# Moving Silus, RG-LRU scans and step-size work within the instruction stream of a hybrid SSD / RG-LRU block

## The chip, the cores and the metric

One core of a Trainium2 chip runs the whole layer as one launch. The metric is the device time of one execution in microseconds (us). The five engines are TensorE (PE), VectorE (DVE), ScalarE (ACT), GpSimd (POOL, idle here) and SyncE (SP, which issues the DMAs). Each engine works through its own instructions in order; semaphores hold an instruction until what it reads is there and what it overwrites has been read.

## What is computed

One layer over 256 latent tokens and 256 context tokens, with 2048 channels, in float32. The normalised and modulated input `h` goes through one projection that is split among two mixers, and both mixers run forwards and backwards:

```python
z, xs, bs, cs, dt_raw, xr, yr = jnp.split(h @ lp['w_in'], IN_SPLITS, axis=-1)
# (A) Mamba-2 SSD: conv + silu of xs, bs, cs; dt = softplus(dt_raw + bias); A = -exp(a_log)
a_cum = jnp.cumsum(dt * A, axis=2)                       # per head and chunk of 128
y_diag = einsum(CB * exp(a_cum_i - a_cum_j), xdt)
y_off  = einsum(C, exp(a_cum), entering_state)
# (B) RG-LRU: r, i = sigmoid(block-diagonal products of conv(xr))
a = exp(-8 * r * softplus(-lam));  u = sqrt(-expm1(2 log a)) * (i * xr);  h_t = a_t h_{t-1} + u_t
```

Then `rmsnorm(y * silu(z))` and `r * gelu(yr)` go through output projections, sigmoid gates merge them, and after one more projection and a gated residual comes a SwiGLU feed-forward network. Context tokens are only needed for the states from which the latent scans start.

## The kernel before

Channels lie on the 128 partitions, tokens in the free dimension: columns 0 to 255 are latent, 256 to 511 context. Almost every product is a *job* (`Job`, line 46): one 128-column tile of a weight matrix, sixteen k-tiles, loaded by DMA in two pieces (`load`, line 150), split by ACT (line 173) and DVE (line 174) into a high and a low part (`parts`, line 164), and multiplied by PE in three passes (`product`, line 177). A ring of four raw and four split pieces runs ahead of PE. A job in the mode "both" has all 512 columns, one in the mode "lat" the 256 latent ones.

PE's order is written out by hand. `run` (line 249) goes through the jobs; behind each job come, in this order: its evacuation (`job.evac`), the next weight pieces, and then the functions that were put off to this place: first those in `turns[0]`, then one `step()` of the queue `bg`. `in_turn(n, f)` called from an evacuation puts `f` behind the n-th job after that one, with n = 0 behind the same job; called from inside a turn, n = 0 is the next job. The order of the other engines is chosen by a list scheduler from the program order and its own estimate of times, with one exception: `fn` (line 105) chains all ACT functions that need a table (Exp, Tanh, Sigmoid, Sqrt, Silu, Gelu) in the order in which the program emits them, so an early one that isn't ready holds all later ones back. ACT loads another table (ACT_TABLE_LOAD) where neighbours of that chain belong to different sets; Exp and Tanh share one here.

Four pieces of this stream matter:

**RG-LRU.** The sixteen channel tiles are handled in eight pairs. `lru_batch` (line 509) puts five steps per pair into `bg`, one behind each job, the fifth together with the next pair's first: `operands(t0)`; the *previous* pair's `scans` (the list `before`); `gates(t0)` and `operands(t1)`; nothing; `gates(t1)` and `decays`. So pair p has its steps behind jobs 4p to 4p+4. `gates` (line 528) issues twelve matmuls into four PSUM banks (lines 535 to 537, tile `lg`), each bank read by one Sigmoid (line 538); the banks of the two directions come from two pools of two and three banks (`lru_ps`, `ssd_ps`), so that a tile's gates need those of the tile before to be read. `decays` are eight Exp and Tanh and six DVE instructions (lines 547 to 550), `scans` (line 552) two Sqrts on ACT, then ten DVE instructions (lines 559 to 565) and two DMAs to `rD`.

**Step sizes.** `dt_evac` (line 598), the evacuation of job 0, computes softplus, cumulative sums and decay weights for 64 heads. `steps(0)` is for the latent tokens, `steps(1)` for the context. Each is a chain of some 30 small instructions on DVE (log1p by a series, lines 132 to 146, then scans, line 614) with one Exp at its head (line 136) and one at its end (line 634 or 641); `turn` (line 645) transposes the results on PE into `wt`, and for part 0 makes `dec` with one more Exp. `steps(0)` is emitted at job 0, its turn and all of `steps(1)` at job 4 (ahead of that job's `step()`), the second turn at job 9.

**SSD.** After the first 34 jobs come four groups of six jobs in the order xs0, C, xs1, B, xs2, xs3 (C is "lat", the others "both"), then 32 gate jobs less those already done, then the z jobs. When a group's xs3 is evacuated (`xs_evac`, line 695), the group's Silus (`silus`, line 723: B, C and the 2048 columns of XS) are emitted, and the rest of its work is put into turns: three context steps, and four *units* (`unit`, line 788), each of a `fetch` (a DMA that broadcasts the cumulative sums from DRAM, line 795, tile AC with two buffers), `operands` (lines 798 to 817: ACT line 804 and DVE line 805 make E, Exp of AC and E, then DVE makes G, line 816) and `products` (PE, line 833, 24 matmuls of 128 columns):

```python
LONG = ((1, 2, 3), (4, 5, 6, 7), (2, 3, 4, 5), (3, 4, 5, 6))       # line 692: context, products, fetch, operands
SHORT = ((2, 3, 5), (7, 9, 11, 13), (4, 6, 7, 9), (5, 7, 9, 11))
```

In groups 0 to 2 the last unit's `operands` are behind the sixth job after xs3. That is the next group's xs3, in whose evacuation the next group's Silus have just been emitted. The last unit's `products` follow one job later, and right behind them comes the next group's `context_tokens` (line 739): transposes of B (`pB`), B times C (`pC`), transposes of XS (`px`, line 736). For group 2 the two jobs after group 3's xs3 are "lat" gate jobs, and with SHORT group 3's `context_tokens` stand behind the second.

Of the kernel before, what the change touches and what calls it, by code (L numbers as in the profile page):

```python
# [10 lines left out]
AF = mybir.ActivationFunctionType  # L11
ALU = mybir.AluOpType
PSUM = bass.MemoryType.PSUM

P = 128
# [4 lines left out]
NG = 4  # L20
# [35 lines left out]
def hybrid_block(  # L56
# [450 lines left out]
    before = []  # L507

    def lru_batch(tiles):
        st = {}  # L510

        def new(name, t):
            st[name, t] = lp.tile([P, 2, 2 * T], F32, tag=name, name=name, bufs=4 if name == "I" else 2)
            return st[name, t]

        def operands(t):

            raw = lp.tile([P, 4, P], F32, tag="lw", name="lw", bufs=1)
            side.dma_start(raw.rearrange("p a b -> p (a b)"), lru_w[t])
            w = [lp.tile([P, 4, P], F32R, tag=n, name=n, bufs=1) for n in ("lh", "ll")]  # L520
            x = [lp.tile([P, 2 * T], F32R, tag=n, name=n, bufs=1) for n in ("xh", "xl")]
            act.copy(w[0], raw)
            dve.tensor_sub(w[1], raw, w[0].bitcast(F32))
            act.copy(x[0], xcs[t])
            dve.tensor_sub(x[1], xcs[t], x[0].bitcast(F32))
            st["op", t] = w, x

        def gates(t):
            R, I = new("R", t), new("I", t)
            (wh, wl), (xh, xl) = st["op", t]  # L530
            for d in range(2):
                for g, (dst, bn) in enumerate(((R, "lba"), (I, "lbx"))):
                    ps = (lru_ps, ssd_ps)[d]("lg")
                    q = 2 * d + g
                    pe.matmul(ps, wh[:, q], xh, start=True, stop=False)  # L535
                    pe.matmul(ps, wh[:, q], xl, start=False, stop=False)
                    pe.matmul(ps, wl[:, q], xh, start=False, stop=True)
                    fn(dst[:, d, :], ps, AF.Sigmoid, bias=col(bn, 16 * d + t))

        def decays():  # L540
            for t in tiles:
                R, I, A, E = st["R", t], st["I", t], new("A", t), new("E", t)
                for d in range(2):
                    n = 16 * d + t
                    fn(A[:, d, :], R[:, d, :], AF.Exp, scale=SL[:, 0, n:n + 1])
                    fn(R[:, d, :], R[:, d, :], AF.Tanh, scale=SL[:, 1, n:n + 1])
                dve.tensor_tensor(E, A, A, ALU.mult)

                dve.scalar_tensor_tensor(E, E, 1.0, R, ALU.add, ALU.mult)
                dve.tensor_tensor(I, I, xcs[t].unsqueeze(1).broadcast_to([P, 2, 2 * T]), ALU.mult)  # L550

        def scans():
            for t in tiles:
                E = st["E", t]
                fn(E, E, AF.Sqrt, bias=epsb[:, 1:2])
            lat, con = slice(0, T), slice(T, 2 * T)
            for t in tiles:
                I, A, E = (st[k, t] for k in "IAE")
                dve.tensor_tensor(I, I, E, ALU.mult)
                dve.tensor_tensor_scan(E[:, 0, con], A[:, 0, con], I[:, 0, con], 0.0, ALU.mult, ALU.add)  # L560
                dve.tensor_tensor_scan(E[:, 0, lat], A[:, 0, lat], I[:, 0, lat],
                                       E[:, 0, 2 * T - 1:2 * T], ALU.mult, ALU.add)
                dve.tensor_tensor_scan(E[:, 1, ::-1], A[:, 1, ::-1], I[:, 1, ::-1], 0.0, ALU.mult, ALU.add)
                ro = tp.tile([P, T], F32, tag="hv", name="ro", bufs=4)
                dve.tensor_tensor(ro.rearrange("p (r c) -> p c r", r=ROWS),
                                  E[:, 0, lat].rearrange("p (c r) -> p c r", r=ROWS),
                                  E[:, 1, lat].rearrange("p (c r) -> p c r", r=ROWS), ALU.add)
                side.dma_start(rD[t], ro)
                del xcs[t]


        t0, t1 = tiles
        todo = [(False, [lambda: operands(t0)]), (False, before[:]), (False, [lambda: gates(t0), lambda: operands(t1)]),
                (False, []), (True, [lambda: gates(t1), decays])]
        before[:] = [scans]
        if tiles[1] == KT - 1:
            todo.append((False, [scans]))
        return todo
# [19 lines left out]
    def dt_evac(ps):  # L598
# [13 lines left out]
        def steps(part):  # L612
            def scan(o, i, n, pr):
                dve.tensor_tensor_scan(o, ones2[pr, :n], i, 0.0, ALU.mult, ALU.add)

            t0, t1, t2, dt = (dp.tile([64, T], F32, tag=f"dt{i}", name=f"dt{i}") for i in range(4))
            da = x[:, part * T:part * T + T]
            log1p_exp(dt, da, (t0, t1, t2))
            dve.tensor_scalar(da, dt, na, None, ALU.mult)
            ones2, ex, ac = t0, t1, t2  # L620
            dve.memset(ones2, 1.0)

            dve.memset(ex, 0.0)
            if part == 0:
                for c in range(2):
                    s = slice(c * P, c * P + P)
                    scan(ac[f, s], da[f, s], P, f)
                    scan(ac[b, s][:, ::-1], da[b, s][:, ::-1], P, b)
                scan(ex[f, 0:P - 1][:, ::-1], da[f, 1:P][:, ::-1], P - 1, f)
                scan(ex[b, 1:P], da[b, P:2 * P - 1], P - 1, b)  # L630
                for c in range(2):
                    for d, pr in enumerate((f, b)):
                        side.dma_start(acD[c, d], ac[pr, c * P:c * P + P])
                fn(ex[:, :P], ex[:, :P], AF.Exp)
                dve.tensor_tensor(ex[f, :P], ex[f, :P], dt[f, 0:P], ALU.mult)
                dve.tensor_tensor(ex[b, :P], ex[b, :P], dt[b, P:2 * P], ALU.mult)
                cols = (dt[:, :P], dt[:, P:], ac[:, :P], ac[:, P:], ex[:, :P])
            else:
                scan(ex[f, :T - 1][:, ::-1], da[f, 1:][:, ::-1], T - 1, f)
                scan(ex[b, 1:], da[b, :T - 1], T - 1, b)  # L640
                fn(ex, ex, AF.Exp)
                dve.tensor_tensor(ex, ex, dt, ALU.mult)
                cols = (ex[:, :P], ex[:, P:])

            def turn():
                pt = ssd_ps("pt")
                for i, src in enumerate(cols):
                    pe.transpose(pt[:, 64 * i:64 * i + 64], src, ident[:64, :64])
                o = 5 * part
                act.copy(wt[:, o:o + len(cols)].rearrange("p a b -> p (a b)"), pt[:, :len(cols) * 64])  # L650
                if part == 0:
                    dve.tensor_scalar(wt[:, 2:4], wt[:, 2:4], -1.0, None, ALU.mult)
                    dg = dp.tile([64, 64], F32, name="dg")
                    dve.tensor_scalar(dg[f], ident[f, :64], ac[f, P - 1:P], None, ALU.mult)
                    dve.tensor_scalar(dg[b], ident[b, :64], ac[b, P:P + 1], None, ALU.mult)
                    pd = ssd_ps("pd")
                    pe.matmul(pd[:, :64], ones[:64], dg, start=True, stop=True)
                    fn(dec, pd[:, :64], AF.Exp)
            return turn

        def first():
            turn0()
            in_turn(4, steps(1))

        turn0 = steps(0)
        in_turn(4, first)

    def start_ssd():
        flush()
# [19 lines left out]

    LONG = ((1, 2, 3), (4, 5, 6, 7), (2, 3, 4, 5), (3, 4, 5, 6))
    SHORT = ((2, 3, 5), (7, 9, 11, 13), (4, 6, 7, 9), (5, 7, 9, 11))

    def xs_evac(g, t):
        def f(ps):
            if (g, t) == (0, 0):
                start_ssd()
            if t == 0:
                sd["XS"] = sd["gp"].tile([P, 4, 2 * T], F32, tag="XS", name="XS", bufs=2)  # L700
            i = 4 * g + t
            conv(ps, sd["XS"][:, t, :].rearrange("p (s t) -> p s t", s=2), col("cw", 4 * i, 4), col("cb", i), 2)
            if t == 3:
                silus, *rest = ssd_group(g)
                silus()
                for ns, fs in zip(LONG if g < NG - 1 else SHORT, rest):
                    for n, part in zip(ns, fs):
                        in_turn(n, part)
        return f

    def ssd_group(g):
# [130 lines left out]
            return products, fetch, operands  # L842

        units = [unit(u, c) for u in range(2) for c in range(2)]
        return (silus, [context_tokens, context_states, carried_states], *zip(*units))

    jobs = [Job(w_dt, KT, "narrow", None, dt_evac)]
    for t in range(N0, KT):
# [155 lines left out]
    first = []  # L1004
# [118 lines left out]
```

## Time and profile before

| | us |
|---|---|
| median of 3 runs | 2028.81 (2024.41 to 2029.35) |
| the profiled execution, own time | 2027.59 |
| its span, first to last instruction | 2025.8 |
| mean granted TensorE clock | 0.986 of full speed |
| PE busy | 1963.7 (97%) |
| DVE busy | 1430.7 (71%) |
| ACT busy | 1088.2 (54%) |

A busy PE is the normal state: what can be won without changing the products is the time in which PE stands, and the time in which it runs at a lower granted clock. In the rows below a line of the timeline gives start and duration in us, engine, line of the kernel, operation, output<-inputs, shape and count; a bracket gives the idle time of that engine just before it and what ended it.

### The profile page before, as it was taken

What the parts mean: (1) busy time and instruction counts of PE and PEld (TensorE: products, weight loads), DVE (VectorE), ACT (ScalarE), POOL (GpSimd) and SP (SyncE); (2) the same over time, 40 slices, a digit from 0 to 9 for tenths busy, and PEclk for the clock granted to TensorE, in tenths of its full rate; (3) what the DMA queues carried; (4) which work ended last, traced back from release to release, by engine and by line L of the source; (5) the groups of instructions that cost most, each with busy time, mean ns of one, the idle gap of its engine ahead of it and who ended that gap; (6) DMA issues with size and microseconds to landing.
All of it is one profiled execution on the core that took longest, in us unless ns stands there. A gap on an engine that the chain in (4) does not pass through costs nothing.

```text
span 2025.8 us, 30510 instructions
## 1 busy us (share of the span) xinstructions
PE 1963.7 (97%) x11633; PEld 1691.9 (84%) x11633; DVE 1430.7 (71%) x2153; ACT 1088.2 (54%) x1652; POOL 0.2 (0%) x4
## 2 busy tenths in 40 slices
PE   7999899999999879999999999899999999999997
PEld 3778898898878769888888888788888888888887
DVE  5578989886776666888777878776666665545544
ACT  4245878684564454766655544554444444444442
POOL 0000000000000000000000000000000000000000
PEclk9999999999999989999999999999999999999999
DMA  9974354556454457899888877577777776666663
GB/s 371 358 271 144 122 160 132 170 170 199 140 160 143 138 164 228 264 315 360 290 274 274 271 249 254 175 249 232 231 241 237 230 230 189 184 188 186 185 193 122
DMA packets 143842, 440.32 MB, mean 217 GB/s; under 512 B 17488, under 2 KB 36176, under 8 KB 143568
## 3 DMA queue, kind: packets, MB, share of 16 engines
q1 hardware_dynamic: 143328, 437.91, 66.4%
q8 instruction: 91, 1.49, 0.3%
q10 hardware_dynamic: 368, 0.47, 0.1%
q14 instruction: 55, 0.45, 0.1%
HBM read 427.77 MB, written 10.55 MB: 216 GB/s over the span
## 4 chain that ended last, share of the span: by engine, by line
PE 92%; DMA 2%; DVE 2%; ACT 2%; issue 1%; SPq 0%; DVEq 0%; ACTq 0%
PE ps L206 36%; PE ps L209 19%; PE ps L188 5%; PE ps L189 5%; PE ps L190 5%; PE ps L192 3%; PE ps L193 3%; PE ps L194 3%; DMA AC<-acD 1%; PE ps L391 1%; PE pa L344 1%; PE ps L392 1%; PE py L833 1%; PE ps L393 1%; PE ps L228 1%; PE lg L535 1%
## 5 line engine op out<-in xcount | busy, mean ns | idle before, releaser
L174 DVE TENSOR_TENSOR wl<-raw,wh 128x1024 fp32r<-128x1024 f32 (+1 forms) x566 | 677.8, 1200 | 386.9 <-ACT wh L173 382.3
L173 ACT CAST wh<-raw 128x1024 fp32r<-128x1024 f32 (+1 forms) x566 | 581.0, 1030 | 646.8 <-issue 221.4
L206 PE MATMUL ps<-T,wh 128*128 128x512 f32 x3236 | 814.7, 393 | 0.0
L206 PEld LDWEIGHTS ps<-T,wh 128*128 128x128 f32 x3236 | 581.6, 189 | 105.2 <-issue 0.7
L209 PEld LDWEIGHTS ps<-T,wl 128*128 128x128 f32 x3236 | 442.7, 190 | 33.3
L209 PE MATMUL ps<-T,wl 128*128 128x256 f32 x3236 | 452.9, 282 | 0.0
L188 PE MATMUL ps<-T,wh 128*128 128x512 f32 x464 | 184.2, 397 | 0.0
L189 PE MATMUL ps<-T,wh 128*128 128x512 f32 x464 | 180.9, 390 | 0.0
L190 PE MATMUL ps<-T,wl 128*128 128x512 f32 x464 | 180.6, 389 | 0.0
L473 DVE SCALAR_TENSOR_TENSOR rawa<-rawa,sc 128x1024 f32<-128x1024 f32 x128 | 153.1, 1222 | 28.4 <-DMA rawa<-in_dram 28.1
L192 PE MATMUL ps<-T,wh 128*128 128x256 f32 x576 | 165.4, 287 | 0.0
L193 PE MATMUL ps<-T,wh 128*128 128x256 f32 x576 | 163.7, 284 | 0.0
L194 PE MATMUL ps<-T,wl 128*128 128x256 f32 x576 | 163.6, 284 | 0.0
L192 PEld LDWEIGHTS ps<-T,wh 128*128 128x128 f32 x576 | 111.3, 193 | 1.9 <-issue 0.7
L193 PEld LDWEIGHTS ps<-T,wh 128*128 128x128 f32 x576 | 111.4, 193 | 1.2 <-issue 0.5
L194 PEld LDWEIGHTS ps<-T,wl 128*128 128x128 f32 x576 | 111.2, 193 | 0.0
L188 PEld LDWEIGHTS ps<-T,wh 128*128 128x128 f32 x464 | 87.1, 188 | 20.5 <-issue 2.3
L189 PEld LDWEIGHTS ps<-T,wh 128*128 128x128 f32 x464 | 87.2, 188 | 18.9 <-issue 1.4
L190 PEld LDWEIGHTS ps<-T,wl 128*128 128x128 f32 x464 | 87.1, 188 | 18.5
L107 ACT ACT_TABLE_LOAD x48 | 61.6, 1283 | 0.8
L804 ACT ACTIVATE E<-AC,wt 128x128 f32<-128x128 f32 x64 | 20.6, 391 | 61.8 <-DMA AC<-acD 61.8
L385 DVE TENSOR_TENSOR wl<-raw,wh 128x896 fp32r<-128x896 f32 x16 | 17.5, 1092 | 45.1 <-ACT wh L384 45.1
(236 smaller groups left out, 1881.8 us busy)
## 6 DMA issues: line engine op xcount, KB each, us to landing
raw<-in_dram SPq DMA_DIRECT2D x534, 512.0 KB, 4.5
rawa<-in_dram SPq DMA_DIRECT2D x128, 512.0 KB, 5.9
wa<-in_dram SPq DMA_DIRECT2D x64, 512.0 KB, 7.2
AC<-acD SPq DMA_DIRECT2D x16, 512.0 KB, 6.6
raw<-in_dram SPq DMA_DIRECT2D x16, 448.0 KB, 7.1
raw<-in_dram SPq DMA_DIRECT2D x16, 384.0 KB, 3.3
raw<-in_dram SPq DMA_DIRECT2D x18, 256.0 KB, 2.7
X<-in_dram SPq DMA_DIRECT2D x8, 512.0 KB, 7.2
```

The costliest lines, as they stand in the source:

```text
L107: i = act.activation(dst, src, func, **kw).ins
L173: act.copy(h[:, :n], raw[:, :n])
L174: held["low"] = dve.tensor_sub(l[:, :n], raw[:, :n], h[:, :n].bitcast(F32)).ins
L188: pe.matmul(ps, wh, T1[:, k, :], start=s, stop=False)
L189: pe.matmul(ps, wh, T2[:, k, :], start=False, stop=False)
L190: pe.matmul(ps, wl, T1[:, k, :], start=False, stop=e)
L192: pe.matmul(ps[:, :T], wh, T1[:, k, :T], start=s, stop=False)
L193: pe.matmul(ps[:, :T], wh, T2[:, k, :T], start=False, stop=False)
L194: pe.matmul(ps[:, :T], wl, T1[:, k, :T], start=False, stop=e)
L206: pe.matmul(ps, wh, job.act(k), start=s, stop=False, skip_group_check=True)
L209: pe.matmul(ps[:, T:], l[:, i % KP, :], job.act(i)[:, :T], start=False, stop=i == last, skip_group_check=True)
L473: i = dve.scalar_tensor_tensor(raw, raw, 1.0, sc[:, h * 1024:h * 1024 + 1024], ALU.mult, ALU.mult, accum_out=MP[:, n, h:h + 1]).ins
```

## The change

The Silus of a group are no longer emitted in the evacuation of xs3 but in a turn with n = 0, behind whatever already stands in that job's turns (for groups 1 to 3 the last unit's `operands`). The scans of a pair go from the second step of the next pair to its third, behind `gates(t0)` and `operands(t1)`. The step-size work is in four turns per run through: `steps(0)` at job 1, its closing Exp and multiplications (`weights`) at job 3, its `turn` at job 5; `steps(1)` at job 7, `weights` at job 9, `turn` at job 11. The last unit of group 2 has its products at the eighth job after xs3 in place of the seventh (`LAST_LONG`), just ahead of group 3's `context_tokens`.

```diff
@@ -570,8 +570,8 @@
 
 
         t0, t1 = tiles
-        todo = [(False, [lambda: operands(t0)]), (False, before[:]), (False, [lambda: gates(t0), lambda: operands(t1)]),
-                (False, []), (True, [lambda: gates(t1), decays])]
+        todo = [(False, [lambda: operands(t0)]), (False, []),
+                (False, [lambda: gates(t0), lambda: operands(t1)] + before), (False, []), (True, [lambda: gates(t1), decays])]
         before[:] = [scans]
         if tiles[1] == KT - 1:
             todo.append((False, [scans]))
@@ -631,16 +631,20 @@
                 for c in range(2):
                     for d, pr in enumerate((f, b)):
                         side.dma_start(acD[c, d], ac[pr, c * P:c * P + P])
-                fn(ex[:, :P], ex[:, :P], AF.Exp)
-                dve.tensor_tensor(ex[f, :P], ex[f, :P], dt[f, 0:P], ALU.mult)
-                dve.tensor_tensor(ex[b, :P], ex[b, :P], dt[b, P:2 * P], ALU.mult)
                 cols = (dt[:, :P], dt[:, P:], ac[:, :P], ac[:, P:], ex[:, :P])
             else:
                 scan(ex[f, :T - 1][:, ::-1], da[f, 1:][:, ::-1], T - 1, f)
                 scan(ex[b, 1:], da[b, :T - 1], T - 1, b)
-                fn(ex, ex, AF.Exp)
-                dve.tensor_tensor(ex, ex, dt, ALU.mult)
                 cols = (ex[:, :P], ex[:, P:])
+
+            def weights():
+                if part == 0:
+                    fn(ex[:, :P], ex[:, :P], AF.Exp)
+                    dve.tensor_tensor(ex[f, :P], ex[f, :P], dt[f, 0:P], ALU.mult)
+                    dve.tensor_tensor(ex[b, :P], ex[b, :P], dt[b, P:2 * P], ALU.mult)
+                else:
+                    fn(ex, ex, AF.Exp)
+                    dve.tensor_tensor(ex, ex, dt, ALU.mult)
 
             def turn():
                 pt = ssd_ps("pt")
@@ -656,14 +660,17 @@
                     pd = ssd_ps("pd")
                     pe.matmul(pd[:, :64], ones[:64], dg, start=True, stop=True)
                     fn(dec, pd[:, :64], AF.Exp)
-            return turn
-
-        def first():
-            turn0()
-            in_turn(4, steps(1))
-
-        turn0 = steps(0)
-        in_turn(4, first)
+                else:
+                    return
+                begin(1)
+
+            in_turn(1, weights)
+            in_turn(3, turn)
+
+        def begin(part):
+            in_turn(1, lambda: steps(part))
+
+        begin(0)
 
     def start_ssd():
         flush()
@@ -689,8 +696,9 @@
 
 
 
-    LONG = ((1, 2, 3), (4, 5, 6, 7), (2, 3, 4, 5), (3, 4, 5, 6))
-    SHORT = ((2, 3, 5), (7, 9, 11, 13), (4, 6, 7, 9), (5, 7, 9, 11))
+    LONG = ((0,), (1, 2, 3), (4, 5, 6, 7), (2, 3, 4, 5), (3, 4, 5, 6))
+    LAST_LONG = LONG[:2] + ((4, 5, 6, 8),) + LONG[3:]
+    SHORT = ((0,), (2, 3, 5), (7, 9, 11, 13), (4, 6, 7, 9), (5, 7, 9, 11))
 
     def xs_evac(g, t):
         def f(ps):
@@ -701,9 +709,8 @@
             i = 4 * g + t
             conv(ps, sd["XS"][:, t, :].rearrange("p (s t) -> p s t", s=2), col("cw", 4 * i, 4), col("cb", i), 2)
             if t == 3:
-                silus, *rest = ssd_group(g)
-                silus()
-                for ns, fs in zip(LONG if g < NG - 1 else SHORT, rest):
+                when = LONG if g < NG - 2 else LAST_LONG if g < NG - 1 else SHORT
+                for ns, fs in zip(when, ssd_group(g)):
                     for n, part in zip(ns, fs):
                         in_turn(n, part)
         return f
@@ -842,7 +849,7 @@
             return products, fetch, operands
 
         units = [unit(u, c) for u in range(2) for c in range(2)]
-        return (silus, [context_tokens, context_states, carried_states], *zip(*units))
+        return ([silus], [context_tokens, context_states, carried_states], *zip(*units))
 
     jobs = [Job(w_dt, KT, "narrow", None, dt_evac)]
     for t in range(N0, KT):
```

## Rows read from the trace of the kernel before

**Rows 1.** The page's first part: busy us, share, instructions of each engine.

```profile
PE 1963.7 (97%) x11633; PEld 1691.9 (84%) x11633; DVE 1430.7 (71%) x2153; ACT 1088.2 (54%) x1652; POOL 0.2 (0%) x4
```

**Rows 2.** Waits of PE, whole span: us in total, times, longest.

```profile
PE py L833 <- DVE G L816: 24.9, 4, 11.6
...
PE lg L535 <- ACT R L107: 7.2, 2, 5.3
```

**Rows 3.** Timeline of PE: the six first matmuls behind those waits.

```profile
199.26 0.50 PE L535 MATMUL lg<-xh,lh 128*128 128x512 f32 x1 [1.89 <-ACT R L107]
...
220.69 0.80 PE L535 MATMUL lg<-xh,lh 128*128 128x512 f32 x1 [5.32 <-ACT R L107]
...
588.13 0.70 PE L833 MATMUL py<-G,xt 128*64 128x128 f32 x4 [5.05 <-DVE G L816]
...
671.77 0.69 PE L833 MATMUL py<-G,xt 128*64 128x128 f32 x4 [6.37 <-DVE G L816]
...
754.61 0.70 PE L833 MATMUL py<-G,xt 128*64 128x128 f32 x4 [11.62 <-DVE G L816]
...
841.80 0.44 PE L833 MATMUL py<-G,xt 128*64 128x128 f32 x4 [1.88 <-DVE G L816]
```

**Rows 4.** Stretches behind the waits: length, PE, PEld, DVE, ACT, POOL busy, PEclk, DMA.

```profile
199.26:203.60 4.34, 4.33 (x13) 3.41 (x14) 1.77 (x2) 4.31 (x6) 0.00 (x0) 0.66 0.00 0
203.60:215.37 11.77, 11.77 (x97) 11.57 (x95) 11.42 (x13) 11.74 (x18) 0.00 (x0) 0.98 0.41 117
...
220.69:225.50 4.81, 4.81 (x13) 3.87 (x14) 4.81 (x7) 3.72 (x7) 0.00 (x0) 0.60 0.16 62
...
588.13:594.00 5.87, 5.87 (x42) 5.54 (x43) 3.97 (x7) 3.43 (x8) 0.00 (x0) 0.57 0.24 42
...
671.77:676.80 5.03, 5.03 (x42) 4.70 (x43) 3.74 (x7) 2.80 (x6) 0.00 (x0) 0.67 0.16 39
...
754.61:764.74 10.13, 10.13 (x74) 9.80 (x75) 2.91 (x4) 1.20 (x3) 0.00 (x0) 0.71 0.26 80
```

**Rows 5.** Timeline of ACT ahead of the first wait for G.

```profile
564.10 1.28 ACT L804 ACTIVATE E<-AC,wt 128x128 f32<-128x128 f32 x4 [1.01 <-DMA AC<-acD]
...
578.79 1.28 ACT L804 ACTIVATE E<-AC,wt 128x128 f32<-128x128 f32 x4 [6.13 <-DMA AC<-acD]
...
581.94 1.92 ACT L107 ACTIVATE XS<-XS 128x2048 f32<-128x2048 f32 x1 [0.93 <-DVE XS L448]
...
585.16 1.06 ACT L107 ACTIVATE AC<-AC 128x1024 f32<-128x1024 f32 x1
```

**Rows 6.** Timeline of ACT ahead of the two waits of the gates.

```profile
196.79 0.42 ACT L107 ACTIVATE dt<-dt 64x256 f32<-64x256 f32 x1 [3.95 <-DVE dt L614]
...
217.49 1.15 ACT L107 ACTIVATE E<-E,epsb 128x1024 f32<-128x1024 f32 x1 [1.15 <-DVE E L549]
...
219.95 0.69 ACT L107 ACTIVATE R<-lg,V 128x512 f32<-128x512 f32 x1
```

**Rows 7.** Stretches of the RG-LRU phase, columns as in rows 4.

```profile
146.00:250.00 104.00, 96.80 (x590) 86.66 (x589) 93.49 (x137) 75.57 (x109) 0.00 (x0) 0.95 0.42 132
250.00:450.00 200.00, 200.00 (x1250) 181.40 (x1249) 174.13 (x194) 159.75 (x219) 0.00 (x0) 1.00 0.51 159
```

**Rows 8.** The page's costliest groups: the table loads.

```profile
L107 ACT ACT_TABLE_LOAD x48 | 61.6, 1283 | 0.8
```

**Rows 9.** Waits of SP, whole span: the queue's stores of the scans.

```profile
SPq L568 <- DVE ro L565: 38.9, 14, 9.7
```

**Rows 10.** Timeline of PE, group 0's first transposes of XS.

```profile
510.63 1.04 PE L736 MATMUL px<-K,XS 128*128 128x128 f32 x8
```

**Rows 11.** Timeline of ACT, the Silus of XS in groups 2 and 3.

```profile
665.59 1.91 ACT L107 ACTIVATE XS<-XS 128x2048 f32<-128x2048 f32 x1 [0.93 <-DVE XS L448]
...
748.43 1.91 ACT L107 ACTIVATE XS<-XS 128x2048 f32<-128x2048 f32 x1 [1.31 <-DVE XS L448]
```

**Rows 12.** Waits between 250 and 500 us: the Sqrts for decays.

```profile
ACT E L107 <- DVE E L549: 1.5, 1, 1.5
```

## The prediction

> **What bounds the kernel.** The first part of the page comes first: PE is busy for 97% of the span, DVE and ACT are well below [rows 1]. So time comes back only where PE stands or runs slowly. The list of waits shows what PE stood for: 24.9 us in four waits for G and 7.2 us in two waits for a gate's Sigmoid [rows 2]. The timeline gives their places: two in the RG-LRU phase, four in the SSD phase [rows 3]. After each of them PE's matmuls take longer. A stretch with a mean granted clock of 0.66 is a mixture of full speed (2.4 GHz) and half speed (1.2 GHz), and costs its length times 0.34 [rows 4].
>
> Next, who makes them late. **The G waits.** For the wait that ends at 588.13, ACT had the last unit's E (line 804) going at 564.10, but that unit's Exp of AC runs only at 585.16. Between them in the chain of table functions stands the next group's Silu of XS at 581.94, which waited for the convolution of the last XS tile; that was late because ACT had first stood 6.13 us for the AC broadcast of a unit of the next group [rows 5]. So a unit that was ready well over 10 us earlier was held by the table order alone. The second and third wait show the same Silu, at 665.59 and 748.43, some 6 us ahead of the end of the wait [rows 3, 11]. The fourth, 1.88 us at 841.80, is among the Silus of the z jobs.
>
> **The gate waits.** Gates of job 6 need the banks of the gates of job 4. The Sigmoids of the latter come in the chain behind the closing Exp of the context's step sizes, which left at 196.79 after 3.95 us of waiting for DVE's scans. The gates of job 8 wait for those of job 6, whose Sigmoid leaves at 219.95, behind the previous pair's second Sqrt, which at 217.49 still waited for DVE [rows 3, 6]. It is one delay: the step sizes make the first Sigmoids late, then the decays, then the Sqrts.
>
> **The change, part by part.** *Silus behind the Exps.* The Silus now stand behind `operands` of the last unit. Nothing is added, and the table loads per group stay two (Exp to Silu and back). The unit's Exps can leave once its E is there, around 568 by estimate (ACT's four pieces end at 565.4, DVE's four follow them), while PE wants G at 583.07 (588.13 less 5.05). So the first three G waits go: 5.05 + 6.37 + 11.62 = 23.04 us [rows 3]. With them goes the slow clock behind them: 5.87 × 0.43 + 5.03 × 0.33 + 10.13 × 0.29 = 2.52 + 1.66 + 2.94 = 7.12 us [rows 4]. The fourth wait stays.
>
> What waits behind the Silus now? On ACT the later Exps, which nobody needs soon. On PE, `context_tokens`, which reads the Silu of XS right behind the products. Without the wait PE gets there sooner. The 5.87 us behind the first wait are 3.35 us at full clock, and the XS transposes are the last 1.04 us of them [rows 4, 10], so PE wants XS some 2.3 us after the products begin: at 585.4, with the Silu done at 583.86 (581.94 + 1.92), and in the second group at 667.7 against 667.50. That leaves 1.5 and 0.2 us [rows 5, 11]. This is the tightest point of the change. What it costs is in no row; the bounds are 0 and, in each of three groups, another landing of AC as late as the 6.13 us of rows 5, which makes 18.4. I take 1.5 us for all three, near the lower end, since the rows as they are would just fit.
>
> *The third group's last unit a job later.* Two "lat" jobs take 11.77 us [rows 4], one 5.9. Its products come one such job later, so XS of group 3 is wanted at about 742.99 + 5.9 + 2.3 = 751.2 and is there at 750.34 [rows 3, 11]. Without the move products and transposes would only lie apart. I cost it at nothing; its two stores are read by the z jobs much later.
>
> *Scans behind the gates, step sizes in four turns.* The closing Exp of either part now comes two jobs behind the head of its DVE chain, so no Sigmoid should wait for a chain just begun; and a gate's first Sigmoids precede the Sqrts. Both waits go: 1.89 + 5.32 = 7.21 us, and the clock behind them: 4.34 × 0.34 + 11.77 × 0.02 + 4.81 × 0.40 = 1.48 + 0.24 + 1.92 = 3.64 us [rows 3, 4]. What it adds is table loads. For seven pairs the Sqrts now part the Sigmoids of t0 and t1, one load more each; the head Exp of the context part comes between Sqrt and Sigmoid, one more. Eight loads of 1.283 us are 10.3 us of ACT [rows 8], but ACT is idle for 40 of 200 us in the steady part and for 28 of 104 in the first [rows 7], and it has a job or two in which to read a bank. Cost: nothing, as long as that holds.
>
> The rows put next to nothing between a load and its neighbours: 0.8 us of idle time over 48 loads [rows 8]. The Trainium skill ("ScalarE: Activation LUTs", sections "What ACT_TABLE_LOAD costs" and "Table sets: the hidden batching unit") says otherwise: it puts a switch at 2.66 us with its drain, and tells one to batch calls by set, which speaks against this change. By that price the eight would be an estimated 21.3 us, still inside ACT's 68 idle us, so the sum stays the same by either price.
>
> The scans' DVE work and their stores move one job later. SP's queue stood for those stores 38.9 us, once 9.7 us [rows 9], and weight loads queue behind them. The list of PE's waits names no load in this phase: the ring of four pieces covers it. If the cover failed once, that 9.7 us would be the cost; the gates and the chain are ahead of it either way, so I take 0. The four stores of the cumulative sums to `acD` also go a job later; their first reader comes with the SSD phase.
>
> *Sum.* 23.04 + 7.12 + 7.21 + 3.64 = 41.0 us, less 1.5 is 39.5. The profiled execution took 2027.59 us by its own time: 2027.6 − 39.5 = 1988.1. The median of the runs is 1.2 us above the profiled one. I say **1989**.
>
> **The rivals.**
> *The Silu of XS takes the place of the Exps.* PE then stands at the transposes. For it: spares of 0.2 to 1.5 us, and the AC landings that stop ACT and DVE in front of XS. Against it: group 0 has no such wait at its transposes [rows 2, 10]. Price up to 18.4 us: 1989 + 18.4 = 2007.
> *DVE becomes the bound of the RG-LRU phase's start.* It has 93.49 us of work in 104 [rows 7]. Take 10.8 us out of this stretch and it is full; what can't wait until after 250, where it idles 26 of 200 us, comes back as a wait for weights. At worst the whole 10.8 is lost: 2000.
> *Slower: the Sqrts stop the second gates of every pair.* They stand now between the two Sigmoid sets. If DVE's last decay product (line 549) of the pair before is later than these jobs, each of seven pairs gets a wait such as the one at 220.69, 5.32 + 1.92 = 7.24 us, 50.7 in all. The old 10.85 go, the 30.2 of the SSD phase are won: 2027.6 + 50.7 − 10.85 − 30.2 = 2037. It decides once that product is some two jobs late (11.8 us by the two "lat" jobs of rows 4); against it, in the steady phase the Sqrts waited for line 549 once, for 1.5 us [rows 12]. The rule of the page named above, batching by set, is the rule against this split; by the row of loads it gets no more than this chance.
> *Nothing happens*, since the scheduler had other reasons for its order: 2028. The chain of table functions is fixed by the program, so this is unlikely.
>
> **How the numbers follow.** Forecast 0.68, the Silu of XS 0.15, DVE 0.10, slower 0.05, nothing 0.02. Every case but the last two is faster by far more than 0.3% (6 us, about what a measurement of this kernel can tell from no change): faster 0.93, same 0.02, slower 0.05. The range goes down to 1981: the full 41.0 without the 1.5, the fourth wait gone too (1.88, and its clock), and 3 us for the spread of the runs. It goes up to 2008, over both partial rivals.
>
> **What would show it.** In the new profile the waits of PE for G should be one of about 2 us, those for R none. The Exps of a last unit should precede the next group's Silu of XS. ACT should have 56 table loads. Near 196 to 225 us the granted clock should be full. A wait of `px` for the Silu of XS, or of `ps` for `wl` before 260 us, would show the first or second rival; waits of `lg` in every pair the third. With the G waits gone and the time above 2010, the reasoning is wrong.

## The result and the profile after

The changed kernel takes 2002.04 us (median of 4 runs, 1999.65 to 2003.36), 0.9871 of the time before, 95% interval 0.9853 to 0.9888. The forecast was 1989 in a range from 1981 to 2008: inside the range, the direction right, but only two thirds of the 39.5 us came. The profiled execution took 2001.06 us; its span is 1999.3 us, 26.5 less than before. Line numbers below are those of the changed kernel; from line 634 on they are up to 8 higher than before (the products are now line 840).

The page's first part and its row of table loads, to be read against [rows 1, 8]:

```profile
PE 1956.0 (98%) x11633; PEld 1684.3 (84%) x11633; DVE 1428.1 (71%) x2153; ACT 1097.1 (55%) x1660; POOL 0.2 (0%) x4
...
L107 ACT ACT_TABLE_LOAD x56 | 71.8, 1283 | 1.0
```

PE's list of waits in the changed kernel, which answers to [rows 2] (us in total, times, longest):

```profile
...
PE pt L652 <- DVE dt L647: 8.0, 1, 8.0
...
PE px L743 <- ACT XS L107: 2.9, 1, 2.9
PE py L840 <- DVE G L823: 1.8, 1, 1.8
...
PE p L772 <- DVE xw L736: 0.8, 1, 0.8
```

The two waits for a gate's Sigmoid are gone, and three of the four waits for G; the fourth, among the z jobs, stands at 1.8 us as before. Three new waits stand in their place. The large one is PE's second turn of the step sizes: two small transposes (tile `pt`) for the context part, which waited 8.0 us for DVE. The smaller is the one named beforehand as the tightest point, PE at the transposes of XS (tile `px`) waiting for the Silu, once. The smallest, 0.8 us at `p`, is a product of the last group's context part that waits for DVE's weighted XS.

What they cost is in the timeline of PE and in the stretches behind them (length, PE, PEld, DVE, ACT, POOL busy, granted clock, DMA):

```profile
247.90 0.47 PE L652 MATMUL pt<-K,dt 64*128 64x64 f32 x2 [8.02 <-DVE dt L647]
...
662.71 0.69 PE L743 MATMUL px<-K,XS 128*128 128x128 f32 x2 [2.94 <-ACT XS L107]
```

```profile
248.30:261.39 13.09, 13.09 (x50) 10.68 (x50) 9.00 (x11) 7.90 (x12) 0.00 (x0) 0.84 0.00 0
662.71:664.70 1.99, 1.99 (x10) 1.99 (x11) 0.00 (x0) 1.98 (x2) 0.00 (x0) 0.50 0.82 286
664.70:671.00 6.30, 6.30 (x52) 6.30 (x52) 5.70 (x10) 5.39 (x13) 0.00 (x0) 0.94 0.72 180
```

At `pt` it is 8.02 us and 13.09 × 0.16 = 2.1 us of clock, 10.1 together; at `px` 2.94 and 1.99 × 0.50 + 6.30 × 0.06 = 1.4, 4.3 together; 0.50 is the lower of the clock's two levels, 1.2 GHz, all through. With the 0.8 us at `p` that makes 15.2. The waits that were to go held 41.0; 41.0 − 15.2 = 25.8 against a measured 26.5, so the account closes to within a microsecond. The page bears it out in another way: PE's idle time fell from 62.1 to 43.3 us (span less busy), PE's busy time by 7.7 us, which is near the 7.3 us that the clock's terms leave (10.8 to come back, 3.5 lost at the new places).

Why was the second turn late? ACT's timeline has the two Exps between which the context's chain of small DVE instructions lies:

```profile
208.91 0.42 ACT L107 ACTIVATE dt<-dt 64x256 f32<-64x256 f32 x1
...
246.97 0.42 ACT L107 ACTIVATE dt<-dt 64x256 f32<-64x256 f32 x1 [6.13 <-DVE dt L614]
```

It took 38.1 us from Exp to Exp. Before it took 16.7: the closing Exp left at 196.79 [rows 6], the head at 180.13, in the kernel before:

```profile
180.13 0.41 ACT L107 ACTIVATE dt<-dt 64x256 f32<-64x256 f32 x1
```

The chain's own instructions are the same. DVE's groups between the two Exps tell the difference, first in the changed kernel (209 to 247 us), then in the kernel before (180.5 to 197.5 us); busy us and mean ns, then idle time:

```profile
L174 DVE TENSOR_TENSOR wl<-raw,wh 128x1024 fp32r<-128x1024 f32 x10 | 12.1, 1208 | 0.0
...
L143 DVE SCALAR_TENSOR_TENSOR dt<-dt,dt 64x256 f32<-64x256 f32 x7 | 2.9, 415 | 0.1
L549 DVE SCALAR_TENSOR_TENSOR E<-E,R 128x1024 f32<-128x1024 f32 x2 | 2.4, 1217 | 0.0
L547 DVE TENSOR_TENSOR E<-A 128x1024 f32<-128x1024 f32 x2 | 2.4, 1216 | 0.0
L563 DVE TENSOR_TENSOR_SCAN E<-A,I 128x512 f32<-128x512 f32 x2 | 2.4, 1190 | 0.0
```

```profile
L174 DVE TENSOR_TENSOR wl<-raw,wh 128x1024 fp32r<-128x1024 f32 x3 | 3.7, 1222 | 0.5 <-ACT wh L173 0.4
L143 DVE SCALAR_TENSOR_TENSOR dt<-dt,dt 64x256 f32<-64x256 f32 x7 | 2.9, 416 | 0.2
```

DVE had next to no idle time in either stretch. The chain's own work is about 10 us in both; the rest of the stretch, some 7 us before and some 28 us now, is other work that stands between its links. Before, the chain's two Exps were neighbours in the table order and held back the gates' Sigmoids, and with them the decays behind a gate. Now the Sigmoids and Exps of a pair stand between the two Exps and are on time, and so are the decays (lines 547, 549) and scans (line 563): a dependent little instruction stands behind one or several of 1.2 us. What was freed for PE was loaded on DVE in the same 40 us. How much of this comes from the freed work as such, and how much from the chain's later place (job 7 in place of 4), no run separates: with the step sizes back at job 4 (third experiment) the chain takes 16.7 us again, from 182.25 to 198.91, but there it holds the Sigmoids again too.

### The profile page after: what moved, and what is told of

It is laid out like the page before. It is cut to its first block, busy times and chain, and to the rows that moved or that the text cites. A ratio compares the mean times of both kernels' runs of the same rounds, so it can differ in the third digit from the quotient of the medians.

```text
span 1999.3 us, 30534 instructions
## 1 busy us (share of the span) xinstructions
PE 1956.0 (98%) x11633; PEld 1684.3 (84%) x11633; DVE 1428.1 (71%) x2153; ACT 1097.1 (55%) x1660; POOL 0.2 (0%) x4
## 4 chain that ended last, share of the span: by engine, by line
PE 92%; DVE 3%; DMA 2%; ACT 2%; issue 1%; SPq 0%; DVEq 0%; ACTq 0%
PE ps L206 37%; PE ps L209 19%; PE ps L188 5%; PE ps L189 5%; PE ps L190 5%; PE ps L192 3%; PE ps L194 3%; PE ps L193 3%; PE ps L391 1%; DMA AC<-acD 1%; PE ps L228 1%; PE pa L344 1%; PE ps L392 1%; PE ps L393 1%; PE py L840 1%
## 5 line engine op out<-in xcount | busy, mean ns | idle before, releaser
L107 ACT ACT_TABLE_LOAD x56 | 71.8, 1283 | 1.0
```

Source lines behind the costliest of these rows:

```text
L107: i = act.activation(dst, src, func, **kw).ins
```

## The experiments

Each run is the changed kernel with one edit, unless told otherwise. Ratios are to the kernel before on the same chip.

**The second turn three jobs later.**

```diff
-            in_turn(3, turn)
+            in_turn(3 if part == 0 else 6, turn)
```

> Only the context part's turn (its two transposes on PE) goes three jobs later, to job 14. Theory A (the turn stands on PE before its chain of small DVE instructions is done, and nothing else is wrong with it): PE's 8.0 us wait at pt goes with the 2.05 us that the next job lost to the clock, nothing takes its place, and the span falls from 1999.3 by about 10 us to 1989. Rival B (the late chain is the trouble, since its closing Exp also holds the Sigmoids of the gates of job 10): the same delay shows as a wait of lg at job 12 of 5 us or more, and the span falls by less than 5 us.

Measured: 1991.0 us, ratio 0.9822 (0.9808 to 0.9837), span 1987.8. PE's waits in the RG-LRU and SSD phases are

```profile
PE px L743 <- ACT XS L107: 2.5, 2, 2.2
...
PE p L772 <- DVE xw L736: 0.9, 1, 0.9
PE py L840 <- DVE G L823: 0.5, 1, 0.5
```

The wait at `pt` is gone and nothing stands in its place. The chain is no faster: its closing Exp leaves at 247.23.

```profile
247.23 0.42 ACT L107 ACTIVATE dt<-dt 64x256 f32<-64x256 f32 x1 [0.78 <-DVE dt L614]
```

So the late chain harms only the turn, not the Sigmoids behind its Exp. Theory A held: the change lost some 10 us because one turn stood too early for the chain that the same change had slowed; three jobs more are enough.

**The scans back ahead of the gates.**

```diff
-(False, []), (False, [lambda: gates(t0), lambda: operands(t1)] + before),
+(False, before[:]), (False, [lambda: gates(t0), lambda: operands(t1)]),
```

> The scans go back to the step ahead of the next pair's gates, all else as in the changed kernel. Theory A (the step sizes were the root of both waits of the gates): no wait of lg for a Sigmoid comes back, table loads fall by about 7, and the context chain, with the first pair's scans out of its way, ends earlier: the wait at pt falls from 8.0 us to 0 to 5; span 1990 to 1997. Rival B (the Sqrts ahead of the gates were a cause of their own): a wait of lg of about 5 us near 200 to 225 us comes back, and the span is 2002 or more.

Measured: 1993.55 us, ratio 0.9836 (0.982 to 0.9853), span 1991.7, 50 table loads. No wait of `lg` came back. The wait at `pt` fell from 8.0 to 0.9 us, since the chain ran from 207.31 to 239.81:

```profile
PE pt L652 <- DVE dt L647: 0.9, 1, 0.9
```

```profile
207.31 0.42 ACT L107 ACTIVATE dt<-dt 64x256 f32<-64x256 f32 x1
...
239.81 0.42 ACT L107 ACTIVATE dt<-dt 64x256 f32<-64x256 f32 x1 [1.19 <-DVE dt L614]
```

That is 32.5 us in place of 38.1. The scans' move did not win the gates' waits; as made, it only slowed the chain, by 5.6 us of the 21.4 that it grew. The rest goes with the step sizes' new places.

**The step sizes back as they were.** The closing Exps and multiplications, too, stand inside `steps` again; those lines are left out here.

```diff
...
-            in_turn(1, weights)
-            in_turn(3, turn)
-        def begin(part):
-            in_turn(1, lambda: steps(part))
-        begin(0)
+            return turn
+        def first():
+            turn0()
+            in_turn(4, steps(1))
+        turn0 = steps(0)
+        in_turn(4, first)
```

> The step-size work is put back as it was (latent part at job 0, context part at job 4), the scans stay behind the gates. Theory A (the step sizes were the root): the first wait of lg, 1.9 us and some clock, comes back, and the second of 5.3 us in part; the wait at pt goes, since the chain again runs at job 4 on a freer DVE. Span 1990 to 1998. Rival B (with the scans behind the gates the old step sizes would have done): no wait of lg over 1 us, span 1989, that is the changed kernel less the 10 us at pt.

Measured: 2001.87 us, ratio 0.9876 (0.9862 to 0.9891), span 2001.1, above what either theory gave. Of the gates' waits the first came back, the second didn't; in its place came two that no kernel had shown, for PSUM banks that ACT had not yet copied (at 221.20 and 236.32):

```profile
PE ps L188 <- ACT pad L440: 2.5, 1, 2.5
PE ps L192 <- ACT gt L487: 2.3, 1, 2.3
PE lg L535 <- ACT R L107: 1.9, 1, 1.9
```

The delay was only passed on. ACT's timeline shows no idle time from the closing Exp at 198.91 to 227.9; the first of the two copies stood in that line among Sigmoids, table loads and Sqrts, and PE stood for it. Which of these pieces made the copies late is not shown. With the run before, this puts the root at the step sizes, as the prediction had it; how it shows depends on what stands next in line.

**Both RG-LRU parts undone**, so that only the Silus and the third group's unit are changed (the two edits above together).

> Step sizes and scans both as before the change; only the Silus and the third group's unit stay changed. Theory A: the two waits of lg come back as they were, 1.9 and 5.3 us, with some 3.6 us of clock, and the wait at pt goes: span 1999.3 - 10 + 10.9 = 2000, so that the two RG-LRU edits together are worth nothing as made. Rival B (the RG-LRU edits won something on balance): 2004 or more.

Measured: 2003.75 us, ratio 0.9871 (0.9855 to 0.9887), the same ratio as the whole change. Its span is 2001.4, between the 2000 and the 2004 of the two theories. The waits of the gates are there, the first again with 1.89 us:

```profile
PE lg L535 <- ACT R L107: 8.8, 2, 6.9
```

So on balance the two RG-LRU edits won nothing that can be measured, and all of the change's gain is the Silus'. Of the four combinations only step sizes in turns with the scans left alone (0.9836) stands out from the others (0.9871, 0.9876, 0.9871).

**The Silus back in the evacuation.**

```diff
-                for ns, fs in zip(when, ssd_group(g)):
+                (silus,), *rest = ssd_group(g)
+                silus()
+                for ns, fs in zip(when[1:], rest):
```

> The Silus are emitted in the evacuation again, the third group's last unit stays a job later. Theory A (the table order alone held the last units): the waits for G of groups 0 and 1 come back with 5.0 and 6.4 us, that of group 2 with 11.6 less the 5.9 us of the job by which it was moved, with some 6 us of clock in all; the 2.9 us wait of px for the Silu of XS goes. Span 1999.3 + 17 + 6 - 4 = 2018. Rival B (other changes of order on ACT and DVE had removed them): less than half of that comes back, span below 2008.

Measured: 2018.42 us, ratio 0.9961 (0.9946 to 0.9976), span 2016.1. Three waits for G are back where they were expected, and `px` doesn't wait. Their places in PE's timeline, and the list:

```profile
588.36 0.48 PE L842 MATMUL py<-G,xt 128*64 128x128 f32 x2 [5.46 <-DVE G L825]
...
670.03 0.48 PE L842 MATMUL py<-G,xt 128*64 128x128 f32 x2 [5.52 <-DVE G L825]
...
753.13 0.48 PE L842 MATMUL py<-G,xt 128*64 128x128 f32 x2 [6.27 <-DVE G L825]
```

```profile
PE py L842 <- DVE G L825: 17.8, 4, 6.3
```

Theory A held: the order of the Silus and Exps in the chain held the last units.

**The third group's last unit at its old job.**

```diff
-                when = LONG if g < NG - 2 else LAST_LONG if g < NG - 1 else SHORT
+                when = LONG if g < NG - 1 else SHORT
```

> The third group's last unit has its products at the seventh job again, all else as in the changed kernel. Theory A (with the Silus behind the Exps that unit is ready in time, so the move is worth nothing): no wait for G near 730 us, the same waits of 2 to 3 us at px elsewhere, span within 2 us of 1999.3. Rival B (the move was needed): a wait for G of 3 us or more behind the seventh job, span 2003 or more.

Measured: 2003.35 us, ratio 0.9872 (0.9855 to 0.9888), no wait for G at that unit. Its span of 2002.3 is 3 us above the changed kernel's, where 2 had been expected at most; the waits at `p` and among the z jobs are 0.3 and 0.4 us longer. By the ratios, the move is worth nothing that can be measured, once the Silus are where they are.

**E's first pieces in the table chain.** What makes the Silu of XS late is a unit of the next group: ACT stands for its AC broadcast, in order, ahead of that Silu. In the changed kernel's third group (timeline of ACT):

```profile
642.82 1.04 ACT L107 ACTIVATE AC<-AC 128x1024 f32<-128x1024 f32 x1
...
645.70 0.63 ACT L107 ACTIVATE B<-B 128x512 f32<-128x512 f32 x1
...
657.60 1.28 ACT L811 ACTIVATE E<-AC,wt 128x128 f32<-128x128 f32 x4 [7.74 <-DMA AC<-acD]
...
660.75 1.91 ACT L107 ACTIVATE XS<-XS 128x2048 f32<-128x2048 f32 x1 [0.93 <-DVE XS L448]
```

The last unit's Exp (642.82) is now well ahead of the next group's Silus, as meant; but the Silu of XS ends at 662.66, when PE has stood 2.9 us. The edit puts the pieces of E into the order of the table functions, so that they can't be issued ahead of that Silu:

```diff
-                    act.activation(E[:, h], AC[:, 0, h], AF.Identity, bias=wt[:, 2 + c, hf:hf + 1])
+                    fn(E[:, h], AC[:, 0, h], AF.Identity, bias=wt[:, 2 + c, hf:hf + 1])
```

> The first pieces of E (the four Identity activations from the AC broadcast) join the chain of table functions, so that those of a next group's unit can't stand on ACT and DVE ahead of the XS convolution and its Silu. Theory A (the landing of AC, waited for in order on ACT and then on DVE, makes the Silu of XS late): the Silu of XS of the third group leaves some 6 us earlier against the job before it, the 2.9 us wait of px goes with 1.4 us of clock, the 8.0 us at pt stays; span 1995. Rival B (DVE or ACT work makes XS late, not the landing): px still waits 2 us or more, span as before.

Measured: 2001.25 us, ratio 0.9861 (0.9847 to 0.9876). The Silu of XS leaves 5.05 us earlier on the clock of the span, at 655.70, and `px` doesn't wait; but the time hardly moved. The last unit among the z jobs now waits longer, 3.0 us in place of 1.8, and the 7.15 us behind that wait ran at a mean granted clock of 0.58, where the changed kernel lost nothing (last section):

```profile
655.70 1.92 ACT L107 ACTIVATE XS<-XS 128x2048 f32<-128x2048 f32 x1 [2.81 <-DVE XS L448]
```

```profile
PE py L840 <- DVE G L823: 3.0, 1, 3.0
```

```profile
813.59:820.74 7.15, 7.15 (x40) 6.10 (x41) 5.28 (x11) 3.55 (x8) 0.00 (x0) 0.58 0.82 256
```

That is 1.2 us of waiting and 7.15 × 0.42 = 3.0 us of clock, against the 4.3 us won at `px`. Theory A's mechanism held, its price didn't: the gain was given back at another place.

**Three edits together**: the later turn, the scans back, all E's in the chain.

> Three edits on the changed kernel: the second turn at job 14, the scans back ahead of the gates, E's first pieces in the chain. Theory A: the waits at pt and px go, none comes in their place, 50 table loads; from the 1991.0 of the run with the later turn alone some 2.5 us of px and 1 us of clock come off: 1987 to 1988. Rival B (the scans' move had a use of its own that the late turn had hidden): a wait of lg or ps returns in the RG-LRU phase, 1991 or more.

Measured: 1991.18 us, ratio 0.9812 (0.9798 to 0.9827). `pt`, `px`, `lg` and `ps` don't wait, yet the 1987 to 1988 weren't reached: the wait for G among the z jobs is 2.7 us, the only one of PE above 1 us left in the two phases, and the 2.77 us behind it ran at a granted clock of 0.51. Neither theory had that.

**Only the first unit's E in the chain**, with the later turn.

```diff
-                    act.activation(E[:, h], AC[:, 0, h], AF.Identity, bias=wt[:, 2 + c, hf:hf + 1])
+                    (fn if u + c == 0 else act.activation)(E[:, h], AC[:, 0, h], AF.Identity,
+                                                           bias=wt[:, 2 + c, hf:hf + 1])
```

> The second turn at job 14, and only each group's first unit has E's first pieces in the chain of table functions, so that the units among the z jobs are as in the changed kernel. Theory A (in the run with all units chained what px gave was taken back by the fourth wait for G, whose E then came behind a z Silu): px does not wait, the wait for G near 805 us is 1.8 us or less, and the time is 2 to 4 us under the 1991.0 of the later turn alone: 1987 to 1989. Rival B (the gain at px is lost in another place, whatever the z jobs do): 1991 again, with a new wait of PE of 2 us or more.

Measured: 1988.23 us, ratio 0.9811 (0.9797 to 0.9824), span 1984.4. `px` doesn't wait, and the wait for G is down:

```profile
PE py L841 <- DVE G L824: 0.4, 1, 0.4
```

That supports theory A: the z jobs' wait came with E in the chain there. The time is in the expected band, though the interval overlaps that of the later turn alone.

**The same with the scans back.**

> The same with the scans ahead of the gates again: 50 table loads in place of 56. Theory A (with the turn out of the way the place of the scans is worth nothing, ACT having room for the loads): the same time within 2 us, no wait of lg. Rival B (six loads or the order of the Sqrts do cost or win something): 3 us or more between the two.

Measured: 1986.86 us, ratio 0.9802 (0.9789 to 0.9815); within 2 us of the one above, no wait of `lg`. The place of the scans is worth nothing measurable once the turn is out of the way, with six table loads less. This is the fastest version seen, some 14 us under the changed kernel by the two ratios.

## Why the prediction came out as it did

**Silus behind the Exps: right.** The three waits for G went, the last unit's Exps precede the Silus, and undoing this part alone brought 17.25 us of waits back (5.46 + 5.52 + 6.27).

**The Silu of XS as the next thing late: right in kind, mis-sized.** The 1.5 us taken for three places came out as 4.3 us, all at the second, the one with the smallest margin (0.2 us by the rows). The 6.13 us for which ACT stood for AC were read at the first place alone; at the second ACT stood 7.46 us in the kernel before, and 7.74 in the changed one:

```profile
662.45 1.28 ACT L804 ACTIVATE E<-AC,wt 128x128 f32<-128x128 f32 x4 [7.46 <-DMA AC<-acD]
```

And the margin was taken with both sides at their old times. With the stops ahead of it gone, PE wanted XS there 7.9 us earlier (659.77 in place of 667.7), but the DMA of AC was issued only 5.0 us earlier (649.29 in place of 654.29) and the Silu ended only 4.8 us earlier (662.66 in place of 667.50). Why the DMA moved by less than PE is not shown. The bound of 18.4 us was far off.

**The later unit: right**, nothing.

**Step sizes and scans: here the prediction failed.** The step that failed is the sentence that the closing Exp "comes two jobs behind the head of its DVE chain, so no Sigmoid should wait". It asked who waits for the Exp on ACT, and left out who waits on PE for what it feeds: the second turn's own transposes, written into PE's order at job 11. Nor did it ask whether the chain keeps its length. The 16.7 us of before were its time on a DVE on which the gates' later work was held back. It took 38.1, and the 10.85 us won at the gates were paid back as 10.1 at `pt`. That the work would have to be fitted into a full DVE was the second rival, priced at 10.8; the price was nearly right, but its place was named as a wait for weights, and no such wait came.

That the time still lay in the range is luck as far as these two edits go: the range reached up to 2008 for the Silu of XS and for DVE's weights, and what filled it was a wait at `pt` that the prediction doesn't have. Of the 13.0 us between the 39.5 forecast and the 26.5 measured, 10.1 are `pt`, 2.8 the mis-sized `px`, 0.8 `p`; the 0.7 us by which these are too many is the same gap as above.

**The scans' part of it: not needed.** The gates' waits had one root, as said; with the scans left in place they don't come back (0.9836). The prediction asked what the edit does to table loads, stores and the second gates, but not what its DVE work does to the chain that now runs beside it: 5.6 us of delay.

**Table loads: right.** 56 as counted, 1283 ns each, 1.0 us of idle time over all of them; ACT's busy time rose by 8.9 us, and the run with six loads less (the last experiment against the one ahead of it) was no slower or faster by more than the measurement tells. The Trainium skill's 2.66 us per switch ("ScalarE: Activation LUTs", "What ACT_TABLE_LOAD costs") doesn't show here: the row has no drain of 1.38 us ahead of a load, and from the end of the Silu at 583.86 to the Exp at 585.16 [rows 5] it is 1.30 us with the load in between. The Trainium skill's rule of batching by set ("ScalarE: Activation LUTs", "Table sets: the hidden batching unit") made no difference that could be measured between 56 and 50 loads. That holds where ACT had the room; in the run with the step sizes back ACT had none for some 29 us, and PE stood 2.5 us for a copy within them.

## What to carry to other kernels

When a stall is removed, the work that it had held back comes at once, and a chain of dependent small instructions that was short in the trace may have been short only because of the stall. For every result that is moved later, list all its readers, above all those in an order that is written by hand, and place them by the time that the chain takes when its engine is full. And undo each part of a compound change alone: here the Silus' part won all that was won, the scans' move cost what the step sizes in turns gained, the unit's move was worth nothing, and one more edit (a turn three jobs later) was worth some 10 us.

## What had not been expected of the hardware

The clock behind a short stop of PE. After waits of nearly equal length the granted clock of the next microseconds differed. The wait of 1.89 us for the gates cost a third of the clock before (0.66 in [rows 4]); the same wait of 1.89 us in the run with both RG-LRU parts undone cost none, at the same place, behind the same work:

```profile
198.69 0.50 PE L535 MATMUL lg<-xh,lh 128*128 128x512 f32 x1 [1.89 <-ACT R L107]
```

```profile
198.69:203.00 4.31, 4.31 (x25) 3.81 (x26) 1.77 (x2) 4.28 (x6) 0.00 (x0) 1.00 0.00 0
```

The wait among the z jobs did the same in reverse: 1.88 us and then a clock of 0.62 in the kernel before, 1.81 us and then 1.00 in the changed one:

```profile
841.80:844.20 2.40, 2.40 (x25) 2.07 (x25) 2.40 (x4) 2.40 (x6) 0.00 (x0) 0.62 0.40 145
```

```profile
817.00:819.00 2.00, 1.91 (x26) 1.70 (x27) 2.00 (x5) 2.00 (x5) 0.00 (x0) 1.00 0.57 212
```

Why they differ is not shown. So the clock's share of a stop of this size can't be read off another stop; some 1.5 us of the 10.8 us of clock in the sum hung on such a stop.
